# Strassen down-weight sums made by DRAM-to-DRAM transfers, and three more gate/up pairs in Strassen form, in a two-layer decoder trunk

## The chip, the core and the metric

One core of one Trainium2 chip runs the whole program. The metric is the device time of one execution in microseconds, as the median of several runs. The profile is one execution with the hardware profiler on; it shows TensorE matmuls (PE) and weight loads (PEld), VectorE (DVE), ScalarE (ACT), GpSimd (POOL), the DMA queues of SyncE (SP), ACT and POOL, and the sixteen DMA engines that all three queues share.

## What is computed

Two decoder layers on 512 tokens of width 1024, in float32. Layer 0 mixes tokens by causal pooling, layer 1 by differential attention with 8 heads. Each mixer is followed by a LayerNorm, a SwiGLU feed-forward block of inner width 2816, and another LayerNorm:

```python
def _swiglu(x, w_gate, w_up, w_down):
    return (jax.nn.silu(x @ w_gate) * (x @ w_up)) @ w_down

for i in range(DEPTH):                    # DEPTH = 2
    h = pool(x) if i % 2 == 0 else diff_attention(x)
    x = layernorm(ALPHA * x + h, ...)
    x = layernorm(ALPHA * x + _swiglu(x, w_gate[i], w_up[i], w_down[i]), ...)
```

## The kernel before

Every float32 operand is split into a high part (rounded to the fp32r type by a copy on ACT) and a low part (the difference, by a subtraction on DVE), and each product is made of three matmuls: high by high, high by low, low by high. All weights lie in DRAM in one array `wall` of chunks of 128 x 1024 (512 KB). SP loads a chunk into one of five `raw` buffers, ACT casts it (a "cast"), DVE subtracts (a "low").

**Gate and up (`ffn`).** The 2816 inner columns are 22 blocks of 128, taken as 11 pairs `k`, a pair being block `k` and block `k + 11`. A pair is made in one of two ways. `plain(f)` makes the gate and the up product of one block, 24 matmuls of 512 columns each, so a pair takes four products. `strassen(k)` makes a pair by seven products, P1, Q5, P6, Q3, P7, P2, Q4 in this order, each of 24 matmuls of 256 columns (a Strassen scheme over halves of the tokens and of the inner rows). Pairs 4 to 10 are Strassen pairs in both layers (`SPLIT`). The seven products share three PSUM banks: P1, P6, P7 and Q4 pile up in bank A, Q5 and Q3 in bank C, P2 has B. Between two products of one bank the value so far is read out: P1, Q5 and P6 by copies on ACT, Q3, P7 and P2 by DVE. The next product of that bank must wait for the read.

A Strassen pair needs seven weight chunks made of four raw ones. Four of the seven are sums of raw chunks on DVE (line 552), so a pair takes 7 lows and 4 sums on DVE, where a plain pair takes 4 lows. The function `ahead` prepares chunks about five products before their use, in an order written out by hand.

The Strassen products also need sums of token quarters of `x`, split into high and low (`xs`). The generator `sums_of_x` makes these on DVE and ACT and is advanced at certain products. The first blocks (three in layer 0, two in layer 1, `early`) run in two halves of the tokens. After the product of a block DVE multiplies (`gated`, line 584), and for the first four blocks it applies gain and bias of the LayerNorm before (`affine`, lines 203 and 204). After each pair `sum_hidden` makes two sums of hidden rows (lines 683 to 690), and ACT's queue stores them in `ssum`.

**Weight sums for the down product.** The down product is a Strassen scheme too, over all rows. Four of its seven weight operands are sums of the four blocks of `w_down`. `load_terms` has POOL load 512 KB pieces (lines 651 and 652, one of each three adding to what lies in the buffer), `weight_sums` adds twice on DVE (lines 657 and 658, 128 x 512 each), and ACT's queue stores the sums to `tsum` in DRAM (line 662). This is done for 11 pieces per layer during gate and up. SP loads the sums from `tsum` in the down phase.

**Order.** The schedule is manual: each engine runs its instructions in the order in which the kernel's code names them, and waits on semaphores only for what an instruction needs. Emission order across engines binds nothing by itself.

Of the kernel before, what the change touches and what calls it, by code (L numbers as in the profile page):

```python
# [18 lines left out]
P = 128  # L19
# [3 lines left out]
DEPTH = 2  # L23
# [29 lines left out]
def trunk(ctx, tc, x, wall, pscale, lam_p, subln, table, lng, lnb, band, first, onehot, out):  # L53
# [386 lines left out]

# [8 lines left out]
    def ffn(layer, late):  # L449
# [5 lines left out]
        with tc.tile_pool(name=f"ffn{layer}", bufs=1) as fp:  # L455
# [6 lines left out]


            order = [k + j * HALF for k in range(HALF) for j in range(2)]
            tsum = dram.tile([4, len(PAIRS), P, 1024], F32, name=f"tsum{layer}")
            ssum = dram.tile([P, 2, 2, HALF, 256], F32, name=f"ssum{layer}")

            def block(i, b):

                if PAIRS[i][1] == 2:  # L470
                    return wall[c1 + 4 * i + b]
                return wall[c1 + 20 + b // 2][:, (b % 2) * 512 : (b % 2 + 1) * 512]


            items = [(p, i) for p in DOWN for i in range(len(PAIRS))]
# [4 lines left out]
            def fetch_item(j):  # L480
                p, i = items[j]
                w = 512 * PAIRS[i][1]
                t = keep.tile([P, 1024], F32, tag="raw", name=f"r{layer}_{j}", bufs=RAWS)[:, :w]
                src = {"P1": 0, "P2": 2, "Q3": 3}
                if p in src:
                    nc.sync.dma_start(out=t, in_=block(i, src[p]))
                else:
                    m = {"Q5": 0, "P6": 3, "P7": 1, "Q4": 2}[p]
                    nc.sync.dma_start(out=t, in_=tsum[m, i, :, :w])
                drops[j] = t  # L490

            def refill():
# [21 lines left out]
            for k in range(HALF):  # L514
                j0 = index[k] = len(chunks)
                c = c0 + 4 * k
                if k in SPLIT:

                    chunks += [(c, ()), (c, (c, c + 1)), (c, (c, c + 2)), (c + 2, ())]
                    chunks += [(c + 1, (c + 1, c + 2)), (c + 3, ()), (c, (c, c + 3))]  # L520
                    step("cast", j0)
                    for w in (
                        "low 0, sum 1, cast 1, sum 4, cast 3, cast 4, low 1, sum 2, cast 2, low 3, "
                        "low 2, sum 6, cast 5, cast 6, low 4, low 5, low 6"
                    ).split(", "):
                        steps.append((w[:-2], j0 + int(w[-1])))
                else:
                    for i in range(4):
                        chunks.append((c + i, ()))
                        step("cast", j0 + i)  # L530
                        step("low", j0 + i)
# [95 lines left out]
                low(3, r3)  # L627
                yield

            terms = {}
            rows_of = hid.rearrange("p (j k) t -> p j k t", j=2)

            def term_slice(k):
                return slice(k % 2 * 512, (k % 2 + 1) * 512)

            def load_terms(k):
                if k < HALF - 1:
                    c = c1 + 4 * (k // 2)  # L640
                    src = wall[c : c + 4][:, :, term_slice(k)].rearrange("(j r) p t -> p j r t", j=2)
                else:
                    src = wall[c1 + 20 : c1 + 22].rearrange("j p (r t) -> p j r t", r=2)
                if k == 1:
                    t = rows_of[:, :, 4:6, :]
                elif k % 2 == 0 and k < HALF - 1:
                    t = rows_of[:, :, 9:11, :]
                else:
                    t = keep.tile([P, 2, 2, 512], F32, tag="gb", name=f"b{layer}_{k}")
                for j in range(2):  # L650
                    nc.gpsimd.dma_start(out=t[:, j], in_=src[:, j])  # L651
                nc.gpsimd.dma_start(out=t[:, 0], in_=src[:, :, 1], accum_op=ALU.add)  # L652
                terms[k] = t

            def sum_terms(k):
                t = terms.pop(k)
                tt(t[:, 1, 1], t[:, 0, 0], t[:, 1, 1], op=ALU.add)
                tt(t[:, 1, 0], t[:, 1, 1], t[:, 1, 0], op=ALU.add)
                yield
                dst = tsum[:, k // 2, :, term_slice(k)].rearrange("(j r) p t -> p j r t", j=2)  # L660
                for j in range(2):
                    nc.scalar.dma_start(out=dst[:, j], in_=t[:, j])
                if k + 2 < HALF - 1 and k != 1:
                    load_terms(k + 2)
                if k == HALF - 2:
                    load_terms(HALF - 1)

            summed_rows = [0]
            behind = []

            def weight_sums():
                g = sum_terms(summed_rows[0])
                summed_rows[0] += 1
                next(g)
                behind.append(g)

            def sum_hidden(k):

# [57 lines left out]
            load_terms(0)  # L736
            load_terms(1)
            sums = sums_of_x()
            for lo in (0, 256):
                for f in range(early):  # L740
                    for i in range(2):
                        product(accs[f][i], 2 * f + i, lo, lo + 256)
                        if not lo and (f, i) in late:
                            late[f, i]()
                        if not lo:
                            advance(2 * early, True)
                    if lo:
                        advance(2 * f + 6)
                        gated(order[f], *accs[f])
                        affine(n - 1, f)  # L750
                        catch_up()
                        if f < 2:
                            weight_sums()
                            next(sums)
                        if f == 1:
                            behind.append(sum_hidden(0))

            def plain(f):
                k = f // 2
                j = index[k] + 2 * (f % 2)  # L760
                a = (bank(f"g{layer}_{f}"), bank(f"u{layer}_{f}"))
                for i in range(2):
# [10 lines left out]
                if f == 3:  # L773
                    load_terms(3)
                if f % 2:
                    behind.append(sum_hidden(k))

            def strassen(k):
# [18 lines left out]
                for j, p in enumerate(GATE):  # L797
# [15 lines left out]
                    if p == "P1":  # L813
                        g0 = tile_of(0)
                        nc.scalar.copy(both(g0), acc)
                    elif p == "Q5":
                        nc.scalar.copy(second, acc)
                    elif p == "P6":
                        nc.scalar.copy(first, acc)
                    elif p == "Q3":  # L820
                        tt(first, acc, first, op=ALU.subtract)  # L821
                    elif p == "P7":
                        tt(second, second, acc, op=ALU.subtract)
                    elif p == "P2":
                        tt(both(g0), acc, both(g0), op=ALU.add)  # L825
                    else:
                        g1 = tile_of(1)
                        nc.scalar.activation(both(g1), acc, AF.Silu)
                    ahead(index[k] + j + 6)
                    catch_up()  # L830
# [5 lines left out]
                if k < HALF - 1:  # L836
                    weight_sums()
                behind.append(sum_hidden(k))

            f = early  # L840
            while f < FB:
                if f // 2 in SPLIT:
                    strassen(f // 2)
                    f += 2
                else:
# [95 lines left out]
    def attention(late):  # L941
        n = 2
        with tc.tile_pool(name="attn", bufs=1) as ap:
# [225 lines left out]
            for h in range(HEADS):  # L1169
# [114 lines left out]
def layout(w):  # L1284
# [10 lines left out]
    def ffn(layer):  # L1295
        g = cols(w["w_gate"][layer], P)
        u = cols(w["w_up"][layer], P)
        for k in range(HALF):
            f = [k, k + HALF]
            if k in SPLIT:  # L1300
# [62 lines left out]
```

## Time and profile before

| | us |
|---|---|
| median of 3 runs | 953.75 (952.97 to 956.2) |
| the profiled execution, its time | 953.15 |
| the profiled execution, its span | 951.3 |
| PE busy in the span | 936.1 (98%) |
| DVE busy in the span | 781.4 (82%) |
| ACT busy in the span | 491.4 (52%) |
| POOL busy in the span | 112.8 (12%) |

The span is cut by stage: pooling to about 38 us, gate and up of layer 0 to 270, down of layer 0 to 386, attention to about 607, gate and up of layer 1 to 837, and down and the last LayerNorm to the end. A matmul's row in the profile has a modelled end that overlaps the next one, so the pace of PE is read from the distance between starts. The same holds for rows of DVE that follow each other without a gap.

### The profile page before, as it was taken

The numbers are of one execution on the slowest core, as the hardware profiler recorded it, in microseconds if no ns is written. First come the engines' busy times: TensorE is split into PE (matmuls) and PEld (weight loads), VectorE is DVE, ScalarE is ACT, GpSimd is POOL, SyncE is SP. The second block draws the span as 40 slices with busy tenths as digits, with TensorE's granted clock in tenths as the row PEclk, the third lists the DMA queues.
The fourth block names the chain that finished last, engine by engine and source line by source line (L and its number), as shares of the span: only waits on it lengthen the run. The fifth ranks groups of instructions, "written<-read, shape, count | busy, mean of one in ns | idle before, by whom it ended". The sixth has DMA issues, their size and how long they took to land.

```text
span 951.3 us, 15381 instructions
## 1 busy us (share of the span) xinstructions
PE 936.1 (98%) x5982; PEld 847.7 (89%) x5982; DVE 781.4 (82%) x1145; ACT 491.4 (52%) x790; POOL 112.8 (12%) x135
## 2 busy tenths in 40 slices
PE   8999999999999999999999999999999999999996
PEld 8898899999988888988888888998899999988884
DVE  6949979999988778688787677779779999987778
ACT  5753335455554457665556553833344554564450
POOL 5311211110001200000000000211111110001101
PEclk9999999999999999999999999999999999999999
DMA  8387998875878964333232222396888885878942
GB/s 220 119 277 244 316 282 260 248 248 205 272 248 266 360 230 134 116 89 97 62 141 79 67 89 89 112 315 199 269 271 246 251 272 208 256 246 278 368 151 90
DMA packets 82248, 197.12 MB, mean 207 GB/s; under 512 B 14804, under 2 KB 26196, under 8 KB 82174
## 3 DMA queue, kind: packets, MB, share of 16 engines
q1 hardware_dynamic: 43052, 115.35, 36.2%
q0 software_dynamic: 15520, 46.14, 17.8%
q10 hardware_dynamic: 23602, 34.63, 10.1%
q8 instruction: 47, 0.77, 0.3%
q14 instruction: 27, 0.22, 0.1%
HBM read 159.38 MB, written 36.72 MB: 206 GB/s over the span
## 4 chain that ended last, share of the span: by engine, by line
PE 92%; DVE 4%; ACT 1%; issue 1%; POOL 0%; DVEq 0%; POOLq 0%
PE A L806 17%; PE P L872 13%; PE C L806 8%; PE Q L872 6%; PE B L806 4%; PE g L126 3%; PE u L125 3%; PE u L126 3%; PE u L127 3%; PE g L127 3%; PE g L125 3%; PE s L1071 2%; PE v L125 2%; PE v L126 2%; PE v L127 2%; PE q L126 2%
## 5 line engine op out<-in xcount | busy, mean ns | idle before, releaser
L552 DVE TENSOR_TENSOR raw<-raw,raw 128x1024 f32<-128x1024 f32 x56 | 68.3, 1219 | 0.5
L107 ACT CAST xs<-hid 128x512 fp32r<-128x512 f32 (+1 forms) x60 | 34.7, 582 | 24.4 <-DVE hid L720 24.4
L108 DVE TENSOR_TENSOR xs<-hid,xs 128x512 fp32r<-128x512 f32 (+1 forms) x60 | 38.5, 642 | 7.8 <-ACT xs L107 7.8
L217 ACT ACTIVATE y<-pt,bT,gT 128x128 f32<-128x128 f32 x96 | 36.1, 456 | 16.7 <-PE pt L212 16.1
L1081 ACT ACTIVATE p<-p,mn 128x128 f32<-128x128 f32 (+3 forms) x64 | 35.4, 554 | 14.9 <-DVE mn L1076 14.9
L584 DVE TENSOR_TENSOR hid<-sg,u 128x512 f32<-128x512 f32 x16 | 11.0, 687 | 30.0 <-PE u L127 19.3
L651 POOL DMA_DIRECT2D b<-in_wall x20 | 14.0, 706 | 170.5 <-DVE g_58l L558 67.6
L712 POOL DMA_DIRECT2D xs<-ssum x24 | 17.4, 725 | 141.4 <-PE Q L872 120.2
L175 POOL TENSOR_TENSOR rs<-rs,mhalf 128x1 f32<-128x1 f32 x16 | 12.2, 767 | 166.4 <-DVE rs L174 126.9
L108 POOL TENSOR_TENSOR sql<-sq,sqh 128x512 fp32r<-128x512 f32 x7 | 9.0, 1290 | 165.3 <-ACT sqh L107 165.3
L108 DVE TENSOR_TENSOR xt<-y,xt 128x512 fp32r<-128x512 f32 x24 | 16.2, 688 | 14.9 <-ACT xt L107 14.9
L651 POOL DMA_DIRECT2D hid<-in_wall x24 | 18.9, 827 | 80.4 <-DMA tsum<-hid 53.0
L1076 DVE CUSTOM_DVE_ANT_0 p<-s,bias 128x128 f32<-128x128 f32 (+3 forms) x64 | 28.1, 485 | 0.0
L688 ACT CAST v<-u 128x512 fp32r<-128x512 f32 x22 | 13.6, 620 | 27.2 <-DVE u L686 27.1
L166 DVE BATCH_NORM_STATS2 st<-res 128x6 f32<-128x512 f32 x32 | 22.2, 695 | 1.1
L832 ACT ACTIVATE sg<-sg 128x512 f32<-128x512 f32 x14 | 8.9, 633 | 25.7 <-DVE sg L825 25.7
L108 DVE TENSOR_TENSOR heads<-k,heads 128x512 fp32r<-128x512 f32 x8 | 5.5, 692 | 20.2 <-ACT heads L107 20.2
L652 POOL DMA_DIRECT2D hid<-in_wall x12 | 14.8, 1232 | 57.6 <-DMA hid<-in_wall 57.6
L600 ACT CAST xs<-hid 128x1024 fp32r<-128x1024 f32 x8 | 8.4, 1051 | 24.1 <-DVE hid L617 11.6
L1095 DVE SCALAR_TENSOR_TENSOR p<-p,sm,p 128x128 f32<-128x128 f32 (+3 forms) x32 | 17.7, 552 | 1.1
L821 DVE TENSOR_TENSOR hid<-C,hid 128x512 f32<-128x512 f32 x14 | 9.7, 691 | 10.8 <-PE C L806 9.2
L107 ACT CAST heads<-k 128x512 fp32r<-128x512 f32 x8 | 4.7, 589 | 26.2 <-PE k L127 26.2
(1118 smaller groups left out, 3738.6 us busy)
## 6 DMA issues: line engine op xcount, KB each, us to landing
raw<-in_wall SPq DMA_DIRECT2D x122, 512.0 KB, 4.5
r<-tsum SPq DMA_DIRECT2D x40, 512.0 KB, 4.1
hid<-in_wall POOLq DMA_DIRECT2D x36, 512.0 KB, 7.2
b<-in_wall POOLq DMA_DIRECT2D x30, 512.0 KB, 5.8
r<-in_wall SPq DMA_DIRECT2D x30, 512.0 KB, 4.3
tsum<-hid ACTq DMA_DIRECT2D x24, 512.0 KB, 5.6
ssum<-v ACTq DMA_DIRECT2D x22, 512.0 KB, 3.7
tsum<-b ACTq DMA_DIRECT2D x20, 512.0 KB, 4.8
```

Of the source, the lines that this page charges most:

```text
L107: nc.scalar.copy(dst_h, src)
L108: (low or nc.vector).tensor_tensor(dst_l, src, dst_h.bitcast(F32), op=ALU.subtract)
L125: nc.tensor.matmul(acc, ah, bh, start=start, stop=False)
L126: nc.tensor.matmul(acc, ah, bl, start=False, stop=False)
L127: nc.tensor.matmul(acc, al, bh, start=False, stop=stop)
L217: nc.scalar.activation(y[:, k, :], pt[:, k * P : (k + 1) * P], AF.Identity, bias=bT[:, n, kk : kk + 1], scale=gT[:, n, kk : kk + 1],)
L552: tt(t, raws[pair[0]], raws[pair[1]], op=ALU.add)
L651: nc.gpsimd.dma_start(out=t[:, j], in_=src[:, j])
L806: nc.tensor.matmul(o, w[:, c], x[:, kk, :], start=p in ("P1", "Q5", "P2") and f + kk + e == 0, stop=p in ("Q4", "Q3", "P2") and (f, kk, e) ...
L872: nc.tensor.matmul(accs[s], x[:, k, r], y[:, c], start=first and k == 0 and e == 0, stop=last and k == m - 1 and e == 2, skip_group_check= ...
L1076: nc.vector.tensor_tensor_reduce(out=p, in0=accs[c][:, :w], in1=biases[h][:, w - 1 :: -1] if w < S else biases[h][:, ::-1], op0=ALU.add, o ...
L1081: nc.scalar.activation(p, p, AF.Exp, bias=mn[:, q, c : c + 1], scale=-1.0, accum_out=sm[:, q, c : c + 1],)
```

## The change

1. The sums of down weights are made by POOL's DMA queue alone, from DRAM to DRAM, with no engine: for each of four sums, six copies (one per row group of `PAIRS`) and then six transfers that add onto the copies. That makes 48 transfers a layer, each of 512 KB, or 256 KB for the last row group. `load_terms`, `weight_sums`, their additions on DVE and their stores on ACT's queue are gone.
2. A generator `terms[layer]` issues them. Layer 0 advances it once per product of gate and up, layer 1 six times per head of attention.
3. Pair 3 of layer 0 and pairs 2 and 3 of layer 1 become Strassen pairs: 8 in layer 0, 9 in layer 1.
4. `sums_of_x` is advanced twice rather than once after each of the first two blocks of layer 1, and from the first plain block on.

```diff
-SPLIT = (4, 5, 6, 7, 8, 9, 10)
+SPLIT = ((3, 4, 5, 6, 7, 8, 9, 10), (2, 3, 4, 5, 6, 7, 8, 9, 10))
...
+    def sum_steps(layer, c):
+        made = sums[layer]
+        for q, start, b in ((0, None, 1), (1, None, 3), (3, 0, 3), (2, 3, 2)):
+            for adds in range(2):
+                for i in range(len(PAIRS)):
+                    if adds:
+                        source, op = block(c, i, b), dict(accum_op=ALU.add)
+                    else:
+                        source, op = made[start][i] if start is not None else block(c, i, q), {}
+                    nc.gpsimd.dma_start(
+                        out=made[q][i], in_=source, max_dma_last_dim=8192, **op
+                    )
+                    yield
...
-            def load_terms(k):
-            ...
-            def sum_terms(k):
-                t = terms.pop(k)
-                tt(t[:, 1, 1], t[:, 0, 0], t[:, 1, 1], op=ALU.add)
-                tt(t[:, 1, 0], t[:, 1, 1], t[:, 1, 0], op=ALU.add)
-            ...
             for lo in (0, 256):
                 for f in range(early):
                     for i in range(2):
                         product(accs[f][i], 2 * f + i, lo, lo + 256)
                         ...
+                        next(terms[layer], None)
                 ...
                         if f < 2:
-                            weight_sums()
-                            next(sums)
+                            for _ in range(1 + layer):
+                                next(xsums)
...
             def plain(f):
                 ...
                 for i in range(2):
                     product(a[i], j + i, 0, S)
+                    next(terms[layer], None)
                     ahead(j + i + 5)
-                    if f >= 3:
-                        next(sums, None)
+                    if f >= early:
+                        next(xsums, None)
                     catch_up()
                 ...
-                if f in (3, 5, 7):
-                    weight_sums()
...
     def attention(late):
                 ...
                 ready(where[0] + 1)
+                for _ in range(3):
+                    next(terms[1], None)
                 ...
                     mix(h - 1)
+                for _ in range(3):
+                    next(terms[1], None)
```

**Where instructions move.** First place: DVE in layer 1 from the multiplication of the fourth block (`sg1_12`) on. Here `g1_Nl` is the low of chunk N, a sum writes `raw`, `u1_1` and `v1_1` are hidden sums of pair 1, and `C1_2` and `A1_2` are the banks of pair 2. Before:

```order
L584 TENSOR_TENSOR hid1_6342<-sg1_12_6766,u1_3_6697 128x512
L203 TENSOR_TENSOR res_67<-res_67,gb2_5243 128x1024
L204 TENSOR_TENSOR res_67<-res_67,gb2_5243 128x1024
L657 TENSOR_TENSOR hid1_6342<-hid1_6342 128x512
L658 TENSOR_TENSOR hid1_6342<-hid1_6342 128x512
L558 TENSOR_TENSOR g1_12l_6758<-raw112_6646,g1_12h_6757 128x1024
L617 TENSOR_TENSOR hid1_6342<-hid1_6342 128x1024
L603 TENSOR_TENSOR xs1_6343<-hid1_6342,xs1_6343 128x1024
```

Now:

```order
L615 TENSOR_TENSOR hid1_6496<-sg1_12_6909,u1_3_6848 128x512
L203 TENSOR_TENSOR res_67<-res_67,gb2_5379 128x1024
L204 TENSOR_TENSOR res_67<-res_67,gb2_5379 128x1024
L583 TENSOR_TENSOR raw108_6671<-raw108_6671,raw111_6747 128x1024
L589 TENSOR_TENSOR g1_12l_6835<-raw109_6680,g1_12h_6834 128x1024
L589 TENSOR_TENSOR g1_13l_6945<-raw111_6747,g1_13h_6944 128x1024
L669 TENSOR_TENSOR u1_1_6954<-hid1_6496 128x256
L670 TENSOR_TENSOR hid1_6496<-hid1_6496 128x256
L671 TENSOR_TENSOR u1_1_6954<-hid1_6496 128x256
L672 TENSOR_TENSOR u1_1_6954<-u1_1_6954,hid1_6496 128x256
L589 TENSOR_TENSOR g1_14l_6948<-raw108_6671,g1_14h_6947 128x1024
L589 TENSOR_TENSOR g1_15l_6988<-raw112_6790,g1_15h_6987 128x1024
```

The sums and lows of the first Strassen pair, which stood four blocks later, now stand right behind the fourth block. All work on `xs` stands ahead of it, and the two additions of the weight sums are gone.

Second place: ACT at the same spot, from the copy of pair 0's hidden sums (`v1_0`) on. `sg1_12` is the silu of the fourth block. Before:

```order
L688 CAST v1_0_6655<-u1_0_6654 128x2x256
L583 ACTIVATE sg1_1_6691<-g1_2_6620 128x512
L555 CAST g1_11h_6724<-raw111_6601 128x1024
L555 CAST g1_12h_6757<-raw112_6646 128x1024
L600 CAST xs1_6343<-hid1_6342 128x1024 x2
L692 DMA ssum1_6345<-v1_0_6655 512x1x256
L583 ACTIVATE sg1_12_6766<-g1_3_6696 128x512
L555 CAST g1_13h_6805<-raw113_6684 128x1024
```

Now:

```order
L674 CAST v1_0_6797<-u1_0_6796 128x2x256
L614 ACTIVATE sg1_1_6842<-g1_2_6764 128x512
L586 CAST g1_10h_6874<-raw108_6671 128x1024
L678 DMA ssum1_6498<-v1_0_6797 512x1x256
L614 ACTIVATE sg1_12_6909<-g1_3_6847 128x512
L797 COPY sg1_2_0_6941<-A1_2_6914 128x512
L586 CAST g1_13h_6944<-raw111_6747 128x1024
L586 CAST g1_14h_6947<-raw108_6671 128x1024
L799 COPY hid1_6496<-C1_2_6915 128x2x256
L586 CAST g1_15h_6987<-raw112_6790 128x1024
L674 CAST v1_1_6955<-u1_1_6954 128x2x256
L801 COPY hid1_6496<-A1_2_6914 128x2x256
```

The copies that read out P1 (`sg1_2_0`), Q5 (from `C1_2`) and P6 (the last row) now stand behind the store of `ssum` and between casts and copies that take a result of DVE.

Third place: POOL in layer 0, right behind the last power of the LayerNorm (`rs_3`); what a row waits for stands in brackets (DMASW are landings of POOL's own transfers). Before:

```order
L175 TENSOR_TENSOR rs_3_505<-rs_3_505,mhalf 128x1 [waits DVE_49,Pool_49]
L651 DMA hid_534<-in_wall 128x2x512 [waits DMAHW4_49,DMAHW6_49,DMAHW0_49,DMAHW7_49,PE_49,Activation_49]
L651 DMA hid_534<-in_wall 128x2x512
L652 DMA hid_534<-in_wall 128x2x512 [waits DMASW0_49]
L651 DMA hid_534<-in_wall 128x2x512 x2
L652 DMA hid_534<-in_wall 128x2x512 [waits DMASW3_49]
L651 DMA hid_534<-in_wall 128x2x512 [waits DMAHW7_49,DMASW2_49,DVE_49]
```

Now:

```order
L175 TENSOR_TENSOR rs_3_505<-rs_3_505,mhalf 128x1 [waits DVE_49,Pool_49]
L470 DMA t_0_0_531<-in_wall 64x2048
L470 DMA t_0_1_532<-in_wall 64x2048
L470 DMA t_0_2_533<-in_wall 64x2048
L470 DMA t_0_3_534<-in_wall 64x2048
L470 DMA t_0_4_535<-in_wall 64x2048
L470 DMA t_0_5_536<-in_wall 128x512
L470 DMA t_0_0_531<-in_wall 64x2048 [waits DMASW0_49]
L470 DMA t_0_1_532<-in_wall 64x2048 [waits DMASW1_49]
```

Before, a load behind the first ones waits for DVE or for a store. Now the 48 rows wait only for landings of POOL's own earlier transfers.

More of the change, by code (lines that the diff above doesn't have):

```diff
@@ L439, in trunk, with block @@
     base = [2]
+    sums = [
+        [
+            [
+                dram.tile([P, 512 * m], F32, name=f"t{layer}_{q}_{i}")
+                for i, (_, m) in enumerate(PAIRS)
+            ]
+            for q in range(4)
+        ]
+        for layer in range(DEPTH)
+    ]
+    def block(c, i, b):
+        if PAIRS[i][1] == 2:
+            return wall[c + 4 * i + b]
+        return wall[c + 20 + b // 2][:, (b % 2) * 512 : (b % 2 + 1) * 512]
+    def sum_steps(layer, c):
[11 more added lines that the diff above has]
+                    yield
+    terms = [
+        sum_steps(layer, base[0] + 2 * FB if layer == 0 else total - FB) for layer in range(DEPTH)
+    ]
     ROWS = [slice(k, k + n) for k, n in PAIRS]
@@ L485, in fetch_item @@
                 if p in src:
-                    nc.sync.dma_start(out=t, in_=block(i, src[p]))
+                    nc.sync.dma_start(out=t, in_=block(c1, i, src[p]))
                 else:
                     m = {"Q5": 0, "P6": 3, "P7": 1, "Q4": 2}[p]
-                    nc.sync.dma_start(out=t, in_=tsum[m, i, :, :w])
+                    nc.sync.dma_start(out=t, in_=sums[layer][m][i])
                 drops[j] = t
@@ L516, in ffn @@
                 c = c0 + 4 * k
-                if k in SPLIT:
+                if k in SPLIT[layer]:
                     chunks += [(c, ()), (c, (c, c + 1)), (c, (c, c + 2)), (c + 2, ())]
@@ L828, in strassen @@
                         nc.scalar.activation(both(g1), acc, AF.Silu)
+                    next(terms[layer], None)
                     ahead(index[k] + j + 6)
+                    next(xsums, None)
                     catch_up()
@@ L841, in ffn @@
             while f < FB:
-                if f // 2 in SPLIT:
+                if f // 2 in SPLIT[layer]:
                     strassen(f // 2)
@@ L1299, in ffn @@
             f = [k, k + HALF]
-            if k in SPLIT:
+            if k in SPLIT[layer]:
                 halves = [m[f][:, :, h : h + 4] for m, h in ((g, 0), (u, 0), (u, 4), (g, 4))]
```

46 lines of the change are left out of this document (1 added, 45 removed).

## The prediction

> **What bounds the kernel now.** I read the page's busy times and its chain first, then who waited for whom on PE, then the starts of PE and DVE around the places that change.
>
> ```profile
> span 951.3 us, 15381 instructions
> PE 936.1 (98%) x5982; PEld 847.7 (89%) x5982; DVE 781.4 (82%) x1145; ACT 491.4 (52%) x790; POOL 112.8 (12%) x135
> PE 92%; DVE 4%; ACT 1%; issue 1%; POOL 0%; DVEq 0%; POOLq 0%
> ```
>
> The chain that ended last runs on PE for 92% of the span. A busy PE need not be a fast one, so the window view (busy us of each engine, then clock, DMA share, GB/s) says whether a Strassen stage has slack:
>
> ```profile
> 97.00:119.00 22.00, 22.00 (x98) 18.22 (x98) 20.80 (x27) 8.12 (x10) 3.92 (x4) 1.00 1.02 341
> 625.40:670.00 44.60, 44.60 (x220) 37.87 (x220) 41.53 (x47) 16.70 (x20) 7.37 (x8) 1.00 0.82 263
> 736.60:756.80 20.20, 20.20 (x171) 20.20 (x170) 19.22 (x24) 10.34 (x13) 2.70 (x3) 1.00 0.88 269
> ```
>
> In all three PE is busy for the whole window at full clock, while DVE stands at 20.80 of 22.00, 41.53 of 44.60 and 19.22 of 20.20 us. So gate and up is bound by PE, with DVE right behind. Work taken from DVE buys nothing here by itself; work brought forward on DVE may cost.
>
> **What PE saves.** The pace is the distance between first starts of products:
>
> ```profile
> 80.06 0.39 PE L125 MATMUL u<-xt,g_7h 128*128 128x512 f32 x1
> 85.50 0.39 PE L125 MATMUL g<-xt,g_8h 128*128 128x512 f32 x1
> 129.19 2.87 PE A L806 x24
> 132.06 2.88 PE C L806 x24
> ```
>
> A plain product takes 85.50 - 80.06 = 5.44 us, a pair of four 21.76. A Strassen product takes 2.88, a pair of seven 20.16. Each converted pair saves 1.60, three save **4.8 us**.
>
> **What DVE must do before the first Strassen pair of layer 1.** Bank A is read by DVE after P7, and Q4 may not start before. DVE works in order, so that read (line 805 now) comes after everything listed ahead of it. I lay DVE's rows end to end from the first multiplication, which PE sets and the change does not move:
>
> ```profile
> 625.37 0.69 DVE L584 TENSOR_TENSOR hid<-sg,u 128x512 f32<-128x512 f32 x1 [4.46 <-PE u L127]
> 625.97 1.22 DVE L203 TENSOR_TENSOR res<-res,gb 128x1024 f32<-128x1024 f32 x1
> 628.37 0.69 DVE L657 TENSOR_TENSOR hid<-hid 128x512 f32<-128x512 f32 x1
> 629.70 1.22 DVE L597 TENSOR_TENSOR hid<-xt 128x1024 f32<-128x1024 f32 x1
> 630.83 1.22 DVE L558 TENSOR_TENSOR g_6l<-raw,g_6h 128x1024 fp32r<-128x1024 f32 x1
> 639.70 0.42 DVE L683 TENSOR_TENSOR u<-hid 128x256 f32<-128x256 f32 x1
> 641.29 1.22 DVE L558 TENSOR_TENSOR g_9l<-raw,g_9h 128x1024 fp32r<-128x1024 f32 x1
> 648.96 0.69 DVE L690 TENSOR_TENSOR v<-u,v 128x512 fp32r<-128x512 f32 x1
> 649.57 1.22 DVE L558 TENSOR_TENSOR g_11l<-raw,g_11h 128x1024 fp32r<-128x1024 f32 x1
> 654.79 0.69 DVE L584 TENSOR_TENSOR hid<-sg,u 128x512 f32<-128x512 f32 x1 [1.61 <-ACT sg L583]
> 696.33 2.87 PE A L806 x24
> ```
>
> From start to start: a multiplication 0.60, an affine 2.40, a 128x1024 step 1.13 to 1.14, the four steps of a hidden sum 1.59, its low 0.61. The two additions of a weight sum took 1.33 (628.37 to 629.70) and are gone. In the new order stand, up to the read after P7: 29 steps of 128x1024 (8 sums of x, 4 lows of xs, 11 lows of chunks 6 to 16, 6 sums of raw chunks), 4 affines, 4 multiplications, 2 hidden sums with their lows, and the reads after Q3 and P7 (0.6 and 0.7). That is 33.1 + 9.6 + 2.4 + 3.2 + 1.2 + 1.3 = 50.8 us, so DVE is done at 625.4 + 50.8 = **676.2**.
>
> PE's side: the first Strassen pair starts eight plain products earlier, 696.3 - 8 x 5.44 = 652.8, and Q4 six products of 2.88 later, at 670.1. DVE is **6.1 us late**. In the old order the same point lay 43.5 us further on, where by the same count DVE had some 15 us less work than time.
>
> To this come waits inside DVE's own row. The last row of the fence but one shows 1.61 us of idling for a silu of ACT; this can happen at the second to fourth multiplication. The bounds are 0 and about 3.4 us; I take 1.2, since a DVE that is behind finds most of its inputs ready. No reason lets DVE go below the sum. So layer 1 loses 6.1 to 9.5, and I take **7.3**. PE will show it in instalments, because ACT stands in the same line:
>
> ```profile
> 653.22 0.52 ACTq L692 DMA_DIRECT2D ssum<-v  x1
> 654.17 0.59 ACT L583 ACTIVATE sg<-g 128x512 f32<-128x512 f32 x1
> ```
>
> The read after P1 is now behind that store, which waits for DVE's low of pair 0, and behind that silu: some 34.0 us of DVE after 625.4 give 659.4, and store, silu and copy 0.5 to 0.6 each give 661.1. P6 would start at 658.5, so it waits 2 to 4 us; Q3 then waits for the read after Q5, which stands behind a cast of the fourth sum; Q4 takes the rest. Behind ACT's late copies stand only casts for chunks that are as late. After this pair DVE needs 19.2 - 1.3 = 17.9 us for 20.2 and catches up 2.3 us a pair, so the next pair should not stall.
>
> **The same in layer 0.** Three early blocks and three plain ones come first, so there is more time:
>
> ```profile
> 63.33 0.69 DVE L584 TENSOR_TENSOR hid<-sg,u 128x512 f32<-128x512 f32 x1 [8.94 <-PE u L127]
> ```
>
> By the same count, 33 steps of 128x1024, 4 affines, 6 multiplications, 3 hidden sums with lows and two reads make 58.7 us: DVE is done at 122.0. The fourth block starts one product before 80.06, at 74.6; the new Strassen pair six later, at 107.3; its Q4 at 124.6. DVE has 2.6 us to spare, and with waits of up to 3.4 it may miss by 0 to 1; I take 0.5.
>
> **The transfers.** In layer 0 all 48 stand on POOL behind nothing but each other, so they do not come one per product: six or more are in flight from about 38 us until all are done. Price, from the page:
>
> ```profile
> q1 hardware_dynamic: 43052, 115.35, 36.2%
> q0 software_dynamic: 15520, 46.14, 17.8%
> hid<-in_wall POOLq DMA_DIRECT2D x36, 512.0 KB, 7.2
> b<-in_wall POOLq DMA_DIRECT2D x30, 512.0 KB, 5.8
> ```
>
> SP's queue moved 115.35 MB in 36.2% of 951.3 us, 335 GB/s of all engines. POOL's took 169.3 us for 46.14 MB, of which 22 adding loads of 512 KB are 11.53 MB; the other 34.6 at 335 GB/s take 103.3 us, which leaves 66.0 us, 175 GB/s, for adding. Per layer the change copies 11.53 MB (34 us) and adds 11.53 MB (66 us): 100 us of all sixteen engines. No row shows a transfer from DRAM to DRAM; the bounds are this and twice this, as each byte meets DRAM on both sides. I take the near end. What it runs beside:
>
> ```profile
> q0 software_dynamic: 4480, 12.58, 34.8%
> q1 hardware_dynamic: 3958, 14.44, 28.9%
> q10 hardware_dynamic: 6464, 9.98, 19.0%
> raw<-in_wall SPq DMA_DIRECT2D x26, 512.0 KB, 5.9
> ```
>
> These are the DMA rows for 38 to 181 us alone. q0 and most of q10 go; the raw chunks' 29% and the hidden sums' 5% stay, so the burst has 66% of the engines and lasts some 150 us, to about 190 (to 340 at the far end). Before, the same engines were 83% busy, over the full in the window 97 to 119, and PE lost nothing with raw chunks landing in 5.9 us. PE needs one raw chunk per 5.0 (20.16 / 4) to 5.4 us, a chunk alone needs 1.6 of the engines, and five buffers stand before it. I take 0.5 us of loss, with 0 and 30 as ends (second rival).
>
> In a sentence apart: the Trainium skill's DMA: Bandwidth & Descriptors, Latency and other measured facts, gives copies between HBM tensors about 207 GB/s, by which the copies would take 56 us (an estimate from that page) and the burst some 30 us longer; no run here shows it yet.
>
> In attention the transfers are spaced by GpSimd's own work:
>
> ```profile
> L108 POOL TENSOR_TENSOR sql<-sq,sqh 128x512 fp32r<-128x512 f32 x7 | 9.0, 1290 | 165.3 <-ACT sqh L107 165.3
> L652 POOL DMA_DIRECT2D hid<-in_wall x12 | 14.8, 1232 | 57.6 <-DMA hid<-in_wall 57.6
> 386.00:567.00 181.00, 180.83 (x1169) 159.31 (x1168) 136.30 (x319) 107.39 (x242) 9.03 (x7) 1.00 0.28 89
> ```
>
> Six issues of at most 1.23 us per head are 7.4 us of the 23.6 (165.3 / 7) that POOL sits idle before each sql; the engines go from 28% to some 83%. sql's result is used a head later. I take 0, with 2 us as the upper end if a landing holds sql up. The removed stores, loads and additions were hidden under PE; they give nothing.
>
> **Sum**, against the profiled 953.15: - 4.8 + 7.3 + 0.5 + 0.5 = **956.65**. The median of the runs is 0.6 higher, so I predict **957.2 us** (0.36% above). Its own range is 954 to 961.
>
> **The rivals.**
> 1. *DVE's lateness is covered, and the saving stands.* It would need DVE to be 4 or more us quicker over 51 us than its rows, or the raw sums ready earlier by ACT. For it: DVE also loses the terms' work just before, and the steady pairs show slack of 2.3. Against: the sum is by rows that stood without gaps. Time 953.75 - 4.8 = 949.0; faster from a loss below 2 us. Chance 0.10.
> 2. *Raw chunks starve in layer 0.* If engines change between queues row by row, a raw chunk of 4 KB rows meets rows of 8 KB: beside adds it takes 1.6 + 2 x 3.0 = 7.6 us where PE needs 5.0 to 5.4. The 66 us of adding stretch to 84, in which 11 chunks come for 16; the missing five cost up to 27 us less what the buffers hold. I put 12 on top: 969. It decides once a chunk lands later than about 10 us. For: DMA share 1.02 above. Against: 5.9 us beside three queues. Chance 0.20. The skill's same page, Queues, rings and completion order, has engines change queues only after whole packets of several descriptors, by which a chunk would wait for a whole transfer of POOL, 3.0 + 1.6 = 4.6 us, and not starve; the 5.9 us above agree with that as well as with the other.
> 3. *Half covered:* the loss in layer 1 is 3 to 5.5 us and nothing is lost in layer 0. 953.75 - 4.8 + 4.5 = 953.5, no change. Chance 0.18.
> The forecast has 0.52.
>
> **Chances and range.** A measurement of this kernel tells about 0.3%, 2.9 us, from no change. The forecast (loss of 5 to 9 in all) lies above that bound three times in five: 0.32 slower, 0.20 the same. With the rivals: faster 0.10, same 0.38, slower 0.52. The range leaves out most of rival 1 and the far half of rival 2: 951 to 971.
>
> **What would show it.** Right: plain products at 5.44 and Strassen ones at 2.88 as before; PE waits at L788 in layer 1 around 655 to 680, named for ACT and DVE, of 6 to 9 us in all, and no other there; DVE without gaps from 625 to 675; q0's share up to about 25%; the 48 transfers of layer 0 done by 190 us, not at the pace of products. Wrong: no wait at pair 2 of layer 1 (rival 1), raw landings above 10 us with PE waiting for casts between 76 and 240 us (rival 2), or PE waiting in attention behind sql.

## The result and the profile after

| | before | after |
|---|---|---|
| median, us (6 runs each, side by side) | 953.36 (952.93 to 956.2) | 961.12 (960.13 to 965.18) |
| ratio of after to before | | 1.0078, 95% interval 1.0062 to 1.0095 |
| the profiled execution, its time, us | 953.15 | 960.84 |
| its span, us | 951.3 | 959.1 |

The change makes the kernel 0.8% slower: 7.8 us, where 3.4 were predicted (957.2 against 953.75). First the page of the kernel after the change: span, busy times, two DMA queues, the chain of waits.

```profile
span 959.1 us, 15738 instructions
...
PE 935.0 (97%) x6198; PEld 856.5 (89%) x6198; DVE 783.0 (82%) x1131; ACT 503.7 (53%) x808; POOL 117.6 (12%) x165
...
q1 hardware_dynamic: 43052, 115.35, 36.9%
q0 software_dynamic: 11264, 57.68, 22.3%
...
PE 79%; DVE 13%; DMA 2%; issue 2%; ACT 2%; SPq 0%; POOL 0%; ACTq 0%; DVEq 0%; POOLq 0%
```

PE's share of the chain fell from 92 to 79%, DVE's rose from 4 to 13%, and a DMA stands in it that was not there. To see where, I cut the span by stage. The timeline of PE gives the first matmul of each stage (start, duration, line, tiles, shape); these are layer 0's gate and up, its down, layer 1's gate and up, its down:

```profile
37.05 0.28 PE L125 MATMUL g<-xt,w2h 128*128 128x256 f32 x1
...
273.86 0.40 PE L854 MATMUL P<-d_0h,xs 128*128 128x512 f32 x1
...
610.61 0.36 PE L125 MATMUL g<-xt,w100h 128*128 128x256 f32 x1
...
845.93 0.40 PE L854 MATMUL P<-d_0h,xs 128*128 128x512 f32 x1
```

The same four starts in the kernel before are 37.31, 270.14, 606.88 and 837.28. Lengths, and what is lost in them when the saving of 1.6 us for each converted pair is set aside:

| stage, us | before | after | difference | saving | lost |
|---|---|---|---|---|---|
| pooling | 37.3 | 37.1 | - 0.3 | | |
| gate and up, layer 0 | 232.8 | 236.8 | + 4.0 | 1.6 | 5.6 |
| down of layer 0, attention | 336.7 | 336.8 | 0.0 | | |
| gate and up, layer 1 | 230.4 | 235.3 | + 4.9 | 3.2 | 8.1 |
| down of layer 1, end | 114.1 | 113.1 | - 0.9 | | |

So the two stages of gate and up hold more than the whole difference. Who PE waited for in them, by the view of waits (us in total, times, the longest):

```profile
PE A L788 <- DVE hid L805: 4.3, 2, 3.8
PE A L788 <- ACT sg L797: 4.1, 1, 4.1
...
PE A L788 <- ACT hid L801: 0.3, 1, 0.3
```

None of these rows exists before. They come to 8.7 us, but 13.7 are lost. The windows around the gaps show the rest (busy us and instructions of PE, PEld, DVE, ACT and POOL, then granted clock, DMA share, GB/s):

```profile
124.30:128.27 3.97, 0.14 (x3) 0.00 (x1) 3.01 (x4) 2.09 (x2) 0.92 (x2) 1.00 1.01 261
128.27:132.74 4.47, 4.47 (x24) 4.47 (x25) 4.44 (x5) 1.41 (x2) 0.50 (x1) 0.62 1.03 286
...
662.20:666.44 4.24, 0.09 (x1) 0.00 (x1) 4.09 (x5) 1.13 (x3) 0.00 (x0) 0.78 0.56 164
666.44:671.78 5.34, 5.30 (x24) 5.10 (x24) 5.31 (x6) 2.48 (x4) 0.00 (x0) 0.54 0.20 70
```

In each layer PE stands for some 4 us, and the 24 matmuls of the next product then run at a mean granted clock of 0.62 and 0.54. Q4 of layer 0's first Strassen pair takes 4.47 us where 2.88 is the rule. Layer 0's loss is 4.0 of gap and 1.6 of slow clock.

**Layer 0's gap.** The chain of waits up to it (start, duration, what; no row left out between the first and the last but queue and issue times below 0.1 us):

```profile
111.82 1.22 DVE raw L583
113.04 1.15 DVE g_16l L589
...
114.24 10.92 DMA raw<-in_wall
...
125.26 1.23 DVE raw L583
126.48 1.14 DVE g_20l L589
127.62 0.61 DVE hid L805
...
128.27 6.80 PE A L788 x42
```

DVE's low at 113.04 frees a raw buffer, SP issues the next chunk at once, and that chunk needs 10.92 us. DVE wants it for a weight sum (line 583) that stands ahead of the read of bank A after P7 (line 805), and idles; its view of waits has one such row:

```profile
DVE raw L583 <- DMA raw<-in_wall: 3.7, 1, 3.7
```

Why the chunk was late stands in the DMA view for 44 to 167 us, the time in which layer 0's 48 transfers ran (GB/s of 40 slices of 3.1 us; then each queue's packets, MB and share of the engines; then issues with their median time to landing):

```profile
GB/s 229 338 388 410 370 304 222 216 213 246 339 413 426 413 282 257 245 214 220 291 418 354 344 219 255 261 263 268 308 392 423 417 393 272 246 236 258 263 314 340
...
q0 software_dynamic: 4032, 23.07, 69.7%
q1 hardware_dynamic: 3422, 12.48, 26.8%
...
t<-in_wall POOLq DMA_DIRECT2D x30, 512.0 KB, 14.2
raw<-in_wall SPq DMA_DIRECT2D x22, 512.0 KB, 10.2
```

The shares of the queues fill the engines, and a raw chunk lands after 10.2 us, where the median of the kernel before is 6.0 in the same stretch. **Layer 1's gap** is another thing: attention has long finished its transfers, no row names a DMA, and DVE works throughout. The windows over the first Strassen pair of each layer, from P1 to the next P1, where 20.16 us are the rule:

```profile
107.00:132.74 25.74, 21.91 (x169) 21.70 (x168) 21.74 (x25) 10.15 (x13) 6.82 (x10) 0.93 1.03 292
656.38:684.65 28.27, 23.34 (x170) 22.52 (x169) 27.88 (x30) 10.64 (x13) 0.00 (x0) 0.88 0.34 112
```

In layer 1 DVE is busy for 27.88 of 28.27 us; in layer 0 for 21.74 of 25.74.

### The profile page after: what moved, and what is told of

It reads as the page before. It is cut to its first block, busy times and chain, and to the rows that moved or that the text cites. A ratio compares the mean times of both kernels' runs of the same rounds, so it can differ in the third digit from the quotient of the medians.

```text
span 959.1 us, 15738 instructions
## 1 busy us (share of the span) xinstructions
PE 935.0 (97%) x6198; PEld 856.5 (89%) x6198; DVE 783.0 (82%) x1131; ACT 503.7 (53%) x808; POOL 117.6 (12%) x165
## 3 DMA queue, kind: packets, MB, share of 16 engines
q1 hardware_dynamic: 43052, 115.35, 36.9%
## 4 chain that ended last, share of the span: by engine, by line
PE 79%; DVE 13%; DMA 2%; issue 2%; ACT 2%; SPq 0%; POOL 0%; ACTq 0%; DVEq 0%; POOLq 0%
PE A L788 19%; PE P L854 13%; PE C L788 9%; PE Q L854 6%; PE B L788 5%; PE s L1053 2%; PE v L125 2%; PE v L127 2%; PE v L126 2%; PE q L126 2%; PE q L127 1%; PE q L125 1%; PE k L125 1%; PE k L127 1%; PE k L126 1%
## 5 line engine op out<-in xcount | busy, mean ns | idle before, releaser
L583 DVE TENSOR_TENSOR raw<-raw,raw 128x1024 f32<-128x1024 f32 x68 | 82.9, 1219 | 4.3 <-DMA raw<-in_wall 3.7
L470 POOL DMA_DIRECT2D t<-in_wall x72 | 51.5, 839 | 54.7 <-DMA t<-in_wall 36.0
L803 DVE TENSOR_TENSOR hid<-C,hid 128x512 f32<-128x512 f32 x17 | 11.7, 691 | 27.2 <-PE C L788 27.2
L175 POOL TENSOR_TENSOR rs<-rs,mhalf 128x1 f32<-128x1 f32 x16 | 12.3, 769 | 163.9 <-DVE rs L174 124.4
L799 ACT COPY hid<-C 128x512 f32<-128x512 f32 x17 | 10.0, 586 | 21.8 <-PE C L788 21.8
L674 ACT CAST v<-u 128x512 fp32r<-128x512 f32 x22 | 13.7, 622 | 13.7 <-DVE u L672 13.7
L615 DVE TENSOR_TENSOR hid<-sg,u 128x512 f32<-128x512 f32 x10 | 6.9, 686 | 16.7 <-PE u L127 13.4
L1053 PE MATMUL s<-heads 64*128 64x256 f32 (+2 forms) x192 | 17.9, 330 | 0.0
```

The lines of the kernel that those rows point to most:

```text
L470: nc.gpsimd.dma_start(out=made[q][i], in_=source, max_dma_last_dim=8192, **op)
L583: tt(t, raws[pair[0]], raws[pair[1]], op=ALU.add)
L1053: nc.tensor.matmul(accs[c][:, :wide], a[r, qs], b[r, :wide], start=i == 0, stop=i == 2)
```

## The experiments

Each kernel below was run beside the kernel before on one chip. The pooling stage ahead of the change took 36.9 to 40.5 us in these profiles, for a reason of its own (last section), which shifts medians by up to 3 us; so the stages are what is compared. The table has the difference of each stage's length from the kernel before, worked out from the same starts as above, in us.

| | median (before beside it) | ratio, 95% interval | pooling | gate and up 0 | gate and up 1 | end |
|---|---|---|---|---|---|---|
| the change | 961.12 (953.36) | 1.0062 to 1.0095 | - 0.3 | + 4.0 | + 4.9 | - 0.9 |
| e1_affine_later | 950.36 (952.81) | 0.9955 to 0.9991 | - 0.5 | + 0.2 | - 3.2 | - 0.9 |
| e2_paced | 956.22 (952.81) | 1.0015 to 1.0049 | + 3.2 | - 1.2 | + 4.9 | - 0.9 |
| e3_sums_alone | 955.87 (952.81) | 0.9995 to 1.0031 | + 3.2 | + 0.8 | 0.0 | - 0.9 |
| e4_eight_eight | 954.48 (952.81) | 1.0001 to 1.0027 | - 0.3 | + 4.9 | - 1.6 | - 0.9 |
| e5_filled | 959.86 (952.85) | 1.0047 to 1.0089 | - 0.2 | + 2.3 | + 5.1 | - 0.9 |
| e6_paced_later | 948.05 (952.85) | 0.9919 to 0.996 | + 0.5 | - 2.2 | - 3.2 | - 0.9 |
| e7_nine_nine | 950.99 (952.85) | 0.9963 to 0.9992 | + 1.5 | + 1.2 | - 3.2 | - 0.9 |

**1. Less DVE work ahead of the first Strassen pair.**

```diff
+            def half_affine(s, i):
+                z = res[:, s, :]
+                op = (ALU.mult, ALU.add)[i]
+                return lambda: tt(z, z, gbs[n - 1][:, i, :], op=op)
+
+            halved = [half_affine(s, i) for s in range(SB) for i in range(2)]
...
-                        affine(n - 1, f)
+                        if layer not in DEFER:
+                            affine(n - 1, f)
...
                     catch_up()
+                if layer in DEFER and SPLIT[layer].index(k) > 0:
+                    for _ in range(2 if layer == 0 and SPLIT[layer].index(k) == 3 else 1):
+                        if halved:
+                            halved.pop(0)()
```

> The change with one edit: the eight DVE steps of 128x1024 that apply gain and bias of the LayerNorm before to the residual (9.6 us of DVE rows) no longer stand between the first products but one by one in the later Strassen pairs, in both layers. The result is unchanged. Theory (in layer 1 DVE is simply too late at the first Strassen pair; the 8.1 us that PE loses there are DVE's work ahead of its read of bank A): 9.6 us less in front of it, so PE waits at most 1 us at pair 2 of layer 1 and the time falls by 7 to 8 us. In layer 0 the theory is that a raw chunk lands late (10.9 us in the chain), not that DVE has too much to do, so DVE's idling for the raw chunk stays and about 4 to 5.6 us are still lost there: about 953.5 us. Rival A (layer 0 is lost to DVE's amount of work as well): both losses go, about 948.5 us. Rival B (layer 1 is lost to ACT's order or to P7's banks, not to DVE's amount): layer 1 still loses 5 or more, 958 us or above.

Layer 1's loss is gone: the stage is 3.2 us shorter than before, the full saving of two pairs. That is DVE's lateness confirmed and rival B out. In layer 0 most went too, which neither the theory nor rival A had right: what is left is 1.75 us (0.15 and the 1.6 saved). One row of PE's waits belongs to it, and one of DVE's names raw chunks:

```profile
PE A L797 <- DVE hid L814: 1.5, 1, 1.5
```

```profile
DVE raw L584 <- DMA raw<-in_wall: 2.6, 2, 2.3
```

The chain puts both long waits at the third Strassen pair, pair 5: a chunk issued at 150.0 us takes 12.93 us there, and Q4 starts late at 166.05. At the first pair PE does not wait at all (DVE waits 0.2 us for a chunk), though the chunks land no sooner than with the change: 12.4 us in the median from 44 to 167 us, 7.9 at least. So at the first pair the late chunk was not enough by itself. It became a gap of 4 us because DVE had nothing to spare.

**2. The transfers of layer 0 spread out.** A small operation on POOL reads a column of a low that DVE has just made, and so holds the next transfer back.

```diff
+            def touch(j):
+                if j < len(chunks):
+                    nc.gpsimd.tensor_tensor(pace, halves[j][1][:, 0:1].bitcast(F32), mhalf, op=ALU.mult)
...
-                    next(terms[layer], None)
                     ahead(index[k] + j + 6)
...
+                    if layer == 0 and j in (0, 2, 3, 5):
+                        touch(index[k] + j + 5)
+                        next(terms[0], None)
```

> The change with one edit: in layer 0 the 48 transfers of the sums no longer run as one burst; ahead of each one from the first plain block on POOL reads a column of the low part of a chunk that is being prepared, so that four go per Strassen pair and one per plain product. The result is unchanged. Theory (layer 0 loses 5.6 us because the burst delays one raw chunk to 10.9 us, DVE waits 3.7 us for it, and the gap in PE halves the clock after it): the raw chunks land in 5 to 7 us again, PE has no gap at the new Strassen pair of layer 0, layer 1 still loses its 8.1 us; about 955.5 us. Rival (DVE had no time to spare there anyway, or the burst costs nothing): the gap stays, 960 to 961 us. Second rival (the burst costs PE and DVE time elsewhere too): below 954 us.

The rows for the same stretch, 44 to 167 us, and PE's waits in gate and up:

```profile
raw<-in_wall SPq DMA_DIRECT2D x22, 512.0 KB, 5.5
t<-in_wall POOLq DMA_DIRECT2D x20, 512.0 KB, 8.1
```

```profile
PE A L795 <- ACT sg L804: 4.1, 1, 4.1
PE A L795 <- DVE hid L812: 0.6, 2, 0.4
```

Raw chunks land in 5.5 us, the wait of 3.8 shrinks to 0.2 (the 0.4 is layer 1's), and layer 0's stage is 1.2 us shorter than before: 0.4 lost of 5.6. Layer 1 keeps its loss to the tenth, and the row that names ACT is layer 1's. The rivals fall. At the first pair of layer 0 either part alone would have done: nothing late, or something to spare. The burst still costs at a later pair when only the second is given (experiment 1).

**3. The sums by transfers, without new Strassen pairs.**

```diff
-SPLIT = ((3, 4, 5, 6, 7, 8, 9, 10), (2, 3, 4, 5, 6, 7, 8, 9, 10))
+SPLIT = ((4, 5, 6, 7, 8, 9, 10), (4, 5, 6, 7, 8, 9, 10))
```

> One part of the change alone: the weight sums by transfers from DRAM to DRAM in both layers, with the Strassen pairs left at 4 to 10 in both layers as before. Theory (the burst alone delays raw chunks, but only a Strassen pair whose chunks are summed during it can starve, and pair 4 comes later with more slack): within 1 us of the kernel before, 952.5 to 954.5 us. Rival (the burst costs by itself, as raw chunks land at 10 us or later): 956 to 959 us, with waits of PE for DVE in layer 0 between 80 and 170 us. Second rival (the removed additions and loads gave something): below 952 us.

The burst is as dense as in the change, and PE has one new wait:

```profile
q0 software_dynamic: 3989, 23.01, 68.8%
...
raw<-in_wall SPq DMA_DIRECT2D x22, 512.0 KB, 10.4
```

```profile
PE A L788 <- DVE hid L805: 0.5, 1, 0.5
```

Here 10.4 us to landing cost 0.8 us in layer 0. The wait is at Q4 of pair 5 again (170.3 us), behind a chunk that took 11.96 us. Experiment 1 has moved steps of DVE in front of that place too, and 1.5 us there rather than 0.5; whether they add to it is not shown. The median of 955.87 lies in the range of the first rival, but 3.2 us of the profiled execution's excess are pooling's; by stage the first theory holds. The removed additions and stores gave nothing in the stages that they left.

**4. One plain pair more in layer 1.**

```diff
-SPLIT = ((3, 4, 5, 6, 7, 8, 9, 10), (2, 3, 4, 5, 6, 7, 8, 9, 10))
+SPLIT = ((3, 4, 5, 6, 7, 8, 9, 10), (3, 4, 5, 6, 7, 8, 9, 10))
```

> The change with pairs 3 to 10 by Strassen's scheme in both layers (pair 2 of layer 1 is plain again). Theory (DVE's work before the first Strassen pair decides in layer 1: with one plain pair more in front it has some 17 us more time for some 8 us more work): no wait at the first Strassen pair of layer 1; the saving is 2 x 1.6 us there and in layer 0, and layer 0 still loses its 5.6 us: 953.4 - 3.2 + 5.6 = 955.8 us. Rival (every early Strassen pair stalls in layer 1, whatever the time in front of it): 6 us or more lost there, 960 us or above.

Layer 1 is 1.6 us shorter than before, with no wait; layer 0 loses 6.5 (4.9 and the 1.6 saved), again by one gap, with a longer slow stretch behind it (a granted clock of 0.50 from 128.2 to 133.6 us):

```profile
PE A L788 <- DVE hid L805: 3.8, 1, 3.8
```

So a Strassen pair in layer 1 is not late in itself. It is late where DVE's list of work is longer than PE's time in front of it.

**5. PE kept busy in its gaps.**

```diff
+                    if FILL.get((layer, k, p)):
+                        w = halves[index[k] + j - 1][0]
+                        hold = bank(f"hold{layer}")
+                        for _ in range(FILL[layer, k, p]):
+                            nc.tensor.matmul(hold[:, :256], w[:, :P], quarter(0, 0, 0)[:, 0, :], start=True, stop=True)
```

> The change with PE's two gaps partly filled: 28 matmuls of 256 columns into a PSUM bank that nobody reads, ahead of Q4 of pair 3 in layer 0 (3.3 us of the gap of 4.0), and 30 ahead of P6 of pair 2 in layer 1 (3.5 us of the gap of 4.3). The result is unchanged; what is added computes nothing. Theory (a gap of about 4 us makes the granted clock fall to 0.5, which costs 1.6 us in layer 0 as nothing else binds there, but nothing in layer 1, where DVE's chain sets Q4): no stretch at 0.5 after the filled gaps, the stage of gate and up of layer 0 is 1.6 us shorter than with the change (down starts 2.4 us later than before rather than 4.0, counted from the start of gate and up), layer 1 is the same within 0.5 us; about 959.5 us. Rival (the clock falls for another reason, for instance at every first Strassen pair): the stretch at 0.5 stays and both stages are as with the change or up to 1 us longer, 961 to 962 us.

The windows at the same places (columns as above):

```profile
124.30:128.27 3.97, 3.80 (x32) 3.59 (x31) 3.27 (x4) 2.10 (x2) 1.01 (x2) 1.00 1.05 268
128.27:131.15 2.88, 2.88 (x26) 2.88 (x26) 2.85 (x3) 1.05 (x1) 0.00 (x0) 1.00 0.95 246
...
664.90:680.00 15.10, 12.90 (x94) 12.69 (x95) 14.96 (x19) 7.30 (x9) 0.00 (x0) 0.89 0.42 136
```

In layer 0 the clock stays at 1.00 and the stage gets 1.7 us shorter, with matmuls that nobody reads in place of a gap. In layer 1 the expectation was half wrong: PE finds its next gap after P6, and the clock still falls (0.89 in the last row). The view of waits has that gap as

```profile
PE C L794 <- ACT hid L805: 2.2, 1, 2.2
```

The stage is as long as with the change, as expected, since DVE's work sets its end: 14.96 of 15.10 us busy.

**6. Both edits together.** The diffs of 1 and 2.

> The change with both edits of the runs before: layer 0's transfers paced by POOL as in e2_paced, and gain and bias of the LayerNorm moved behind the first Strassen pairs in both layers as in e1_affine_later. The result is unchanged. Theory (the saving of PE, 3 x 1.6 us, is there as counted, and only DVE's lateness and the late raw chunk ate it): no wait of PE in gate and up of either layer, down of layer 0 starts 1.6 us earlier than in the kernel before and layer 1's gate and up is 3.2 us shorter, and with the 0.9 us that all changed kernels gain at the end 952.8 - 1.6 - 3.2 - 0.9 = 947.1 us (947 to 948). Rival (pacing adds waits of POOL that reach PE later, or the affine steps hurt the later pairs): above 949.5 us.

The windows of the first Strassen pair in each layer:

```profile
107.20:127.40 20.20, 20.20 (x170) 20.18 (x169) 16.91 (x20) 9.22 (x11) 4.77 (x8) 1.00 0.89 231
651.20:671.40 20.20, 20.20 (x170) 20.20 (x169) 19.69 (x23) 9.82 (x12) 0.00 (x0) 1.00 0.48 159
```

PE is busy throughout at full clock. The median is 948.05 us, 0.5% below the kernel before, and this version beats both. By stages it is the saving as counted: three pairs by 1.6, and 0.9 at the end. The further 0.6 in layer 0 lie ahead of the pair, 0.5 of them in PE's first wait of the stage (0.2 us rather than 0.7), and pooling is 0.5 longer. That the median is 0.95 above the 947.1 expected is not taken apart further.

**7. One pair more in layer 0.**

```diff
-SPLIT = ((3, 4, 5, 6, 7, 8, 9, 10), (2, 3, 4, 5, 6, 7, 8, 9, 10))
+SPLIT = ((2, 3, 4, 5, 6, 7, 8, 9, 10), (2, 3, 4, 5, 6, 7, 8, 9, 10))
...
-                        if f < 2:
-                            for _ in range(1 + layer):
+                        if f < 3:
+                            for _ in range(2):
```

> As e6_paced_later, with pair 2 of layer 0 by Strassen's scheme too (9 pairs in both layers; the sums of x are advanced twice after each of the three early blocks). The result is unchanged. The count of DVE's rows that the prediction used, for this pair: from the first multiplication (63.3 us) 29 steps of 1.14, four multiplications, two hidden sums with lows and two reads make 41.2 us, so DVE is done at 104.5 at the earliest and with some 2 us of waits at 106.5; PE would start Q4 at about 102.8. Theory (the count decides where the first Strassen pair may stand): PE loses 2 to 4 us there and gains 1.6, so 0.5 to 2.5 us slower than e6_paced_later. Rival (with the transfers paced there is room for one more): 1.6 us faster than e6_paced_later, with no wait of PE at pair 2 of layer 0.

The window of pair 2 in layer 0:

```profile
86.97:111.49 24.52, 21.21 (x169) 20.41 (x168) 24.32 (x27) 12.12 (x15) 5.76 (x11) 1.00 0.67 231
```

The pair takes 24.52 us in place of 20.16, a loss of 4.4 where 2 to 4 were expected. DVE is busy for 24.32 of it. PE's longest wait there, for ACT as in layer 1, leaves the clock at 1.00:

```profile
PE C L804 <- ACT hid L815: 2.0, 1, 2.0
```

Layer 0 is 3.3 us longer than in 6. The median is 2.9 us above that of 6, a little more than the 0.5 to 2.5 expected; its interval against the kernel before ends just short of no change. The row count found the side and nearly the size.

## Why the prediction came out as it did

**The saving** of 4.8 us was right. With the losses removed (6), both layers show it in full.

**Layer 1** was right in mechanism and near in size: 8.1 us lost, 7.3 predicted, inside its bounds of 6.1 to 9.5. The instalments came as described in part: P6 waited 4.1 us for ACT, Q3 not at all, P7 0.3, and Q4 only 0.5, last and behind DVE. These waits make 4.9 us, where 6 to 9 were to be seen. DVE's read of bank A stands in the chain of the kernel after as

```profile
681.03 0.61 DVE hid L805
```

The prediction had it done at 676.2 and 1.2 of waits; layer 1 starts 3.7 us later than before (610.61 - 606.88), which makes 681.1, and the row ends at 681.6. One thing was not foreseen: after PE's 4.2 us the clock fell to 0.54 as a mean over P6, which adds 2.5 us to that product and so took the place of waits. It cost little, because DVE's work set the end anyway: with the gap partly filled (5) the stage stayed as it was.

**Layer 0 is the step that failed.** Two terms of 0.5 us stood for it, one for a DVE that "has 2.6 us to spare" and one for the raw chunks ("I take 0.5 us of loss"); together they measured 5.6. DVE's own term held. It waited 2.0 us for silus, inside the 3.4 allowed, and without the late chunk it would have been done with the read at about 124.5 us (128.2 less 3.7), as PE came free at 124.4: nothing was spare, and little was missing. Experiment 2, with no chunk late, shows the same as 0.2 us of waiting and 0.4 of loss.

The term of the raw chunks is the one that failed: the other 5.2 us or so. One late chunk made DVE wait 3.7 us, and all of it reached PE; Q4's slow clock, which no term had and which experiment 5 took back, added 1.6. The first mistake was to price the chunk by PE's need of one per 5.0 to 5.4 us, apart from DVE, which had no room left for a delay. With 9.6 us of room (experiment 1) the same pair has no gap. The second was the sentence "five buffers stand before it". A sum holds two raw buffers until its low is done, and the chain shows SP issuing the late chunk in the moment that a buffer came free, 7.3 us before DVE wanted it: 6.0 us to landing would have been in time, 10.9 was not.

On the clock, the Trainium skill's TensorE: Matmul & The Clock Gate, Part 1: The HAM clock gate, has PE fall to half rate after an idle window of about 3.4 us. Both gaps here, 4.0 and 4.2 us, agree with that. Of two shorter ones, 2.2 us in experiment 5 was followed by a lower clock, which does not agree, and 2.0 us in experiment 7 was not.

**The transfers** were mis-sized the other way. The prediction had 100 us of all engines for a layer's 48 and an end by about 190; the row of q0 gives 69.7% of 123 us, 85.7 us (269 GB/s for copies and adds together), and they ended by 167. The slices of the DMA view alternate between some 400 GB/s and 215 to 260, four times over, as the four rounds of copies and adds do; that fits adding as the slow half, but was not tried apart. That they come as one burst was right. Denser meant later raw chunks: 10.2 us, above the 7.6 that the second rival had worked out for engines that change between queues row by row, and far above the 4.6, an estimate of mine from the rule of whole packets in the Trainium skill's DMA: Bandwidth & Descriptors, Queues, rings and completion order. Neither way of counting held with more than one transfer ahead.

**The rivals.** The second (raw chunks starve) named the right sign, landings above 10 us, and too large a price: 12 us, for sixteen chunks that were to fall behind one after the other. In experiment 3 the same landings cost 0.8 us, and in the change one chunk made one gap, which needed a DVE with nothing to spare. The first and third had layer 1 quicker than its rows; it was not. Attention cost nothing, as taken.

**The end** of every changed kernel is 0.9 us shorter, in no term of the sum. The last store is issued and the span ends 3.8 us after the start of this row, against 4.7 before (timelines of SP's queue of the kernel after and of the kernel before):

```profile
955.32 0.99 SPq L837 DMA_DIRECT2D out<-res  x2
```

```profile
946.67 1.06 SPq L855 DMA_DIRECT2D out<-res  x2
```

It comes with the sums by transfers (experiment 3 has it too); why is not shown. By stages the account closes: - 4.8 + 5.6 + 8.1 - 0.9 - 0.3 (pooling) = 7.7 of the 7.8 us between the spans. Against the sum of the prediction (956.65, profiled 960.84) layer 0 is 4.6 us over and layer 1 0.8, and the end and pooling, which no term had, take off 1.2.

## What to carry to other kernels

Delays that end on one engine's ordered list are not priced one by one: add up all that stands ahead of the decisive instruction, waits included, and compare the sum with the time in front of it. A list with nothing to spare passes a late input on in full (here 3.7 us). When a step on a full engine is moved earlier, look for work on the same list that nobody needs yet, and move that behind (here 9.6 us of gain and bias). Transfers that waited for nothing but each other ran as one burst here (48 issued from 44 to 149 us); a small operation ahead of each, which reads a fresh result, held them to the pace of the work beside them (to 258 us).

## What the runs showed of the hardware

The pooling stage, which no edit touches before 37 us, began in more than one way. The windows of the kernel before and of e2_paced, both at a listed clock of 1.00:

```profile
10.00:14.00 4.00, 4.00 (x23) 3.25 (x23) 2.76 (x5) 1.70 (x4) 0.81 (x1) 1.00 1.04 370
```

```profile
10.00:14.00 4.00, 4.00 (x14) 2.92 (x14) 2.83 (x5) 1.73 (x4) 0.78 (x1) 1.00 1.04 335
```

PE is busy in both, but passes 23 matmuls in one and 14 in the other; by the start of gate and up this is 3.2 us. It could account for most of the spread of single runs (951.4 to 956.44 us in 31 runs of the kernel before), and a difference of 3 us between medians wants the stages beside it. What decides it, these runs do not show. In experiment 7 PE also passes 14 matmuls in this window, and there the listed clock is 0.50; so the 1.00 listed for e2_paced may not be what PE ran at, which is not shown either. And with copies from DRAM to DRAM beside raw loads the engines moved up to 426 GB/s in a slice, above the 335 that the prediction had taken from loads into SBUF and the 370 of the first window above.
